# A dense projection stage with weight pieces made the moving operand, 512 columns at a time

## The chip, the cores and the metric

One NeuronCore of one Trainium2 chip runs the whole program. The metric is device time in microseconds of one execution, lower is better. Before the change the median of three runs is 1664.23 us (1663.21 to 1665.11).

## What is computed

One decoder layer over 256 tokens of width 2048, everything in float32:

```
h = x @ w_in                        # 2048 -> 9216: u, v, q, k, vb, gate_a, gate_b
v = LayerNorm(gelu(hv)); ya = (gelu(hu) * (tril(W_s) v + b_s)) @ w_out_a
ob = stick_breaking_attention(q, k, vb) @ w_out_b           # 8 heads of 128
x = LayerNorm(alpha*x + (sigmoid(ga)*ya + sigmoid(gb)*ob) @ w_o)
x = LayerNorm(alpha*x + top2_of_16_experts(x) + sigmoid(x @ w_g) * (p @ w_p))
```

The change touches the first four lines, called the dense part below. The router, the experts and the last norm keep their code.

## The kernel before

**Pieces.** Every dense weight is streamed from HBM once, in 2 MB tiles of 128 partitions by 4096 floats, through a pool of 12 such tiles that also holds activations (`B`, `load_one`, `prefetch`, lines 45 to 147). A load is issued on SP's queue as soon as a tile comes free (`done`). A tile is cut into eight pieces of 128x512. `split_next` (lines 235 to 252) turns each piece into two parts in the float32r format: ACT copies the piece into `hi` (L247), DVE subtracts to get `lo` (L248). Four piece buffers (`pc`) rotate, and `next_piece` keeps three pieces ahead of TensorE.

**Products.** A float32 product is made of three float32r products, hi*hi, hi*lo and lo*hi. A piece holds two 128-row chunks of 256 output columns, and costs 12 matmuls of 256 moving columns, in one of two forms. In `ws_piece` (L261) the 128x128 weight block is stationary and 256 tokens move, so the result comes out transposed (channels on partitions, tokens along the free dimension). In `xs_piece` (L275) a block of 128 tokens is stationary and 256 weight columns move, so the result has tokens on partitions. `block` runs eight pieces into one PSUM bank.

**Order.** vb (xs), then q and k alternating (ws), v (xs), u (ws), then eight rounds of gate_a, gate_b, w_out_a, w_out_b (all ws), then w_o (xs). After every second piece `pop_bg` issues one entry of a queue of small background jobs: attention steps `att1`, `att2`, `att3`, the norm of v, and `gate` (L413), which makes the causal product of one head, adds a bias that varies along the free dimension (`bsB`), multiplies by `uT`, and splits the result into `yax`. Each merge round ends with two DVE products, one POOL sum (L449) and an ACT/DVE split into `mixh`, `mixl`.

**Behind it.** After w_o come the norm, the router and the expert loop (L722, L748), which also streams 2 MB tiles.

Of the kernel before, what the change touches and what calls it, by code (L numbers as in the profile page):

```python
# [8 lines left out]
F32 = mybir.dt.float32  # L9
# [4 lines left out]
OP = mybir.AluOpType  # L14
# [18 lines left out]
def trunk(ctx, tc, I, out):  # L33
# [22 lines left out]
    def MM():  # L56
        return psum.tile([128, 512], F32, name="mm", tag="mm")
# [12 lines left out]
    def spec(key, parts):  # L70
        loads.append((key, parts))
# [3 lines left out]
    def spec_in(kind, i, base):  # L75
        spec((kind, i), [(slice(0, 4096), w_in[base + i].rearrange("p c f -> p (c f)"))])

    for i in range(4):
        spec_in("vb", i, 16)
    for i in range(4):  # L80
        spec_in("q", i, 8)
        spec_in("k", i, 12)
    for i in range(4):
        spec_in("v", i, 4)
    for i in range(4):
        spec_in("u", i, 0)
    for i in range(8):
        spec_in("ga", i, 20)
        spec_in("gb", i, 28)
        spec(("ab", i), [(slice(0, 2048), w_oa[i].rearrange("p c f -> p (c f)")),  # L90
                         (slice(2048, 4096), w_ob[i].rearrange("p c f -> p (c f)"))])
    for i in range(8):
        spec(("wo", i), [(slice(0, 4096), w_o[i].rearrange("p c f -> p (c f)"))])
# [73 lines left out]
    for a, b in ((0, 2), (2, 4), (4, 8), (8, 12), (12, 16)):  # L167
        s = slice(a * 256, b * 256)
        SP.dma_start(xr[:, s], I["xT"][:, a:b, :].rearrange("p c t -> p (c t)"))
        SP.dma_start(w0[:, s], w_in[16, :, a:b, :].rearrange("p c f -> p (c f)"))  # L170
    tiles["vb", 0] = w0
    w1 = B("w1")
    for i in range(4):
        SP.dma_start(w1[:, i * 1024:(i + 1) * 1024], w_in[17, :, 4 * i:4 * i + 4, :].rearrange("p c f -> p (c f)"))
    tiles["vb", 1] = w1
# [41 lines left out]

    vbv = B("vbv").rearrange("p (k a f) -> p k a f", k=2, a=2)
# [16 lines left out]
    def split_next():  # L235
        i = psplit["i"]
        if i >= len(psplit["list"]):
            return
        k, p = psplit["list"][i]
        psplit["i"] += 1  # L240
        if p == 0:
            cur[k] = take(k)
        if k == ("vb", 0):
            xsplit(2 * p)
        w = cur[k][:, p * 512:(p + 1) * 512]
        hi, lo = pc[:, 0, i % 4, :], pc[:, 1, i % 4, :]
        ACT.activation(hi, w, AF.Copy)  # L247
        DVE.tensor_sub(lo, w, hi.bitcast(F32))  # L248
        if p == 7:
            cur.pop(k)  # L250
            done()
        pieces.append((hi.rearrange("p (c f) -> p c f", c=2), lo.rearrange("p (c f) -> p c f", c=2)))
# [8 lines left out]
    def ws_piece(ps, p, rh, rl, first, last, c0):  # L261
        hi, lo = next_piece()
        n = 0
        for c in range(2):
            for j in range(2):
                js = slice(j * 128, (j + 1) * 128)
                o = ps[:, j * T:(j + 1) * T]
                for l, r in ((hi, rh), (hi, rl), (lo, rh)):
                    PE.matmul(o, l[:, c, js], r[:, c0 + c, :], start=(first and n == 0),  # L269
                              stop=(last and c == 1 and l is lo), skip_group_check=True)  # L270
                    n += 1
        if p % 2:
            pop_bg()

    def xs_piece(ps, p, sh, sl, first, last, c0):  # L275
        hi, lo = next_piece()
        n = 0
        for c in range(2):
            for a in range(2):
                as_ = slice(a * 128, (a + 1) * 128)  # L280
                o = ps[:, a * 256:(a + 1) * 256]
                for l, r in ((sh, hi), (sh, lo), (sl, hi)):
                    PE.matmul(o, l[:, c0 + c, as_], r[:, c, :], start=(first and n == 0),  # L283
                              stop=(last and c == 1 and l is sl), skip_group_check=True)
                    n += 1
        if p % 2:
            pop_bg()

    def block(f, ops_h, ops_l):
        ps = MM()  # L290
        for p in range(8):
            f(ps, p, ops_h, ops_l, p == 0, p == 7, 2 * p)
        return ps

    plan([("vb", i) for i in range(4)])
    for i in range(4):
        plan([("q", i), ("k", i)])
    plan([("v", i) for i in range(4)])
    plan([("u", i) for i in range(4)])
    for i in range(8):  # L300
        plan([("ga", i), ("gb", i), ("ab", i)])
    plan([("wo", i) for i in range(8)])
# [45 lines left out]
    for i in range(4):  # L348
        ps = block(xs_piece, xh, xl)
        DVE.tensor_copy(vbv[:, 0, :, i * 256:(i + 1) * 256], ps.rearrange("p (a f) -> p a f", a=2))  # L350
    for i in range(4):
        ps = block(ws_piece, xh, xl)
        ACT.activation(qk[:, 0, 2 * i:2 * i + 2, :].rearrange("p h t -> p (h t)"), ps, AF.Copy, scale=SCALE)
        ps = block(ws_piece, xh, xl)
        DVE.tensor_copy(qk[:, 1, 2 * i:2 * i + 2, :].rearrange("p h t -> p (h t)"), ps)
        att_bg(2 * i)
    state["reserve"] = 1
    for i in range(4):
        ps = block(xs_piece, xh, xl)
        DVE.tensor_copy(vbv[:, 1, :, i * 256:(i + 1) * 256], ps.rearrange("p (a f) -> p a f", a=2))  # L360
# [5 lines left out]
    uT = ug[:, 0:2048].rearrange("p (h t) -> p h t", h=NH)  # L366
# [5 lines left out]
    bsB = vbv[:, 0, 1, :].rearrange("p (h t) -> p h t", h=NH)  # L372
    SP.dma_start(wsT, I["gmlp_ws"])
    SP.dma_start(bsB.rearrange("p h t -> p (h t)"), I["gmlp_bs"].to_broadcast([128, 1024]))
# [34 lines left out]
    for i in range(4):  # L409
        ps = block(ws_piece, xh, xl)  # L410
        ACT.activation(uT[:, 2 * i:2 * i + 2, :].rearrange("p h t -> p (h t)"), ps, AF.Gelu_apprx_tanh)

    def gate(h):  # L413
        f = AUX()
        for a in range(2):
            PE.matmul(f[:, a * 128:(a + 1) * 128], v[:, a, h * 128:(h + 1) * 128], wsT[:, h, :],
                      start=True, stop=True)
        y = S("y")
        DVE.tensor_tensor(y[:, 0:256].rearrange("p (a t) -> p a t", a=2),
                          f[:, 0:256].rearrange("p (a t) -> p a t", a=2),  # L420
                          bsB[:, h:h + 1, :].to_broadcast([128, 2, 128]), op=OP.add)
        DVE.tensor_mul(y[:, 0:256], y[:, 0:256], uT[:, h, :])
        ACT.activation(yax[:, 0, h, :], y[:, 0:256], AF.Copy)
        DVE.tensor_sub(yax[:, 1, h, :], y[:, 0:256], yax[:, 0, h, :].bitcast(F32))

    drain()
    for h in range(NH):
        bg.append(lambda h=h: gate(h))
# [3 lines left out]
    for i in range(8):  # L432
        sg = []
        for k in range(2):
            ps = block(ws_piece, xh, xl)
            t = S("sg")
            ACT.activation(t, ps, AF.Sigmoid)
            sg.append(t)
        if i == 0:
            drain()  # L440
            free(2)
            mixh = B("mixh", F32R).rearrange("p (c t) -> p c t", c=DC)
            mixl = B("mixl", F32R).rearrange("p (c t) -> p c t", c=DC)
        for k, src in ((0, yax), (1, obx)):
            ps = MM()
            for p in range(4):
                ws_piece(ps, p, src[:, 0], src[:, 1], p == 0, p == 3, 2 * p)
            DVE.tensor_mul(sg[k], sg[k], ps)
        POOL.tensor_add(sg[0], sg[0], sg[1])  # L449
        mh = mixh[:, 2 * i:2 * i + 2, :].rearrange("p c t -> p (c t)")  # L450
        ml = mixl[:, 2 * i:2 * i + 2, :].rearrange("p c t -> p (c t)")
        ACT.activation(mh, sg[0], AF.Copy)
        DVE.tensor_sub(ml, sg[0], mh.bitcast(F32))
# [16 lines left out]
    lst = C("lst", [128, 2, 8, 6])  # L470
# [4 lines left out]
    for i in range(8):  # L475
        ps = block(xs_piece, mixh, mixl)
        xb = x1[:, :, i * 256:(i + 1) * 256]
        DVE.scalar_tensor_tensor(xb, xb, ALPHA, ps.rearrange("p (a f) -> p a f", a=2), op0=OP.mult, op1=OP.add)
        for a in range(2):
            DVE.bn_stats(lst[:, a, i, :], x1[:, a, i * 256:(i + 1) * 256])  # L480
        if i == 4:
            DVE.tensor_tensor(rwg, rw, gc[:, 0, :, None].to_broadcast([128, DC, 32]), op=OP.mult)
# [544 lines left out]
def _lay(inputs):  # L1027
    import numpy as np
    a = {k: np.asarray(v) for k, v in inputs.items()}

    def cols(w, c, n):
        return w.reshape(c, 128, n, 256).transpose(2, 1, 0, 3)
# [11 lines left out]
        "w_in": cols(a["w_in"][0], DC, 36),  # L1044
        "w_out_a": cols(a["w_out_a"][0], 8, 8),
        "w_out_b": cols(a["w_out_b"][0], 8, 8),
        "w_o": cols(a["w_o"][0], DC, 8),
# [3 lines left out]
        "gmlp_bs": a["gmlp_bs"].reshape(1, 1024),  # L1051
# [30 lines left out]
```

## Time and profile before

| | |
|---|---|
| median of three runs | 1664.23 us |
| profiled execution | 1663.73 us |
| its span, first to last instruction | 1661.70 us |
| dense part on TensorE | 5.35 to 629.3 us |
| router | 629.3 to 647 us |
| experts, last norm, output | 647 to 1661.7 us |

The span is what the trace covers; some 2 us lie around it. TensorE's matmuls overlap in the trace: one of 256 columns is shown with 0.28 us although the next starts 0.12 us later. The pace is therefore read from start to start, not from the duration. A float32 matmul is recorded as two instructions, a float32r one as one.

### The profile page before, as it was taken

To read this page: it belongs to the slowest core of one execution; us is meant where nothing else is said; L and a number is where in the kernel's file an instruction comes from. 1 tells how busy PE (TensorE), PEld (TensorE's weight loads), DVE (VectorE), ACT (ScalarE), POOL (GpSimd) and SP (SyncE) were. 2 spreads that over 40 slices of the span, in tenths; PEclk is the share of its full clock that TensorE was granted. 3 is DMA by queue.
4 is the path that set the end of the run, shared out by engine and by line. 5 is a ranking of instruction groups with operands and counts; after the bars stand their busy time and mean duration, and the time that the engine had idled before them with its cause. 6 is when DMAs were issued, how large, how long until landed. Compare 5 with 4: busy or idle time off the path is not lost. (4 is left out here: it accounts for less than half of the span.)

```text
span 1661.7 us, 23179 instructions
## 1 busy us (share of the span) xinstructions
PE 1616.9 (97%) x9974; PEld 1064.9 (64%) x9974; DVE 558.1 (34%) x1016; ACT 391.7 (24%) x696; POOL 38.6 (2%) x41
## 2 busy tenths in 40 slices
PE   8999999999999999999999999999999999999994
PEld 8999999999999995433333333553535535455323
DVE  5555576555555663120212131012010120101126
ACT  5455455444444441100001100000000000000001
POOL 0000000000000000000000000000000000000012
PEclk9999999999999999999999999999999999999997
DMA  9724553445546856999999999999998998998994
GB/s 387 322 102 153 207 199 129 176 165 190 192 164 254 316 195 263 394 412 414 428 427 428 427 428 427 427 426 424 387 429 374 381 427 375 428 382 373 429 387 173
DMA packets 44191, 540.94 MB, mean 326 GB/s; under 512 B 7090, under 2 KB 7090, under 8 KB 10546
## 3 DMA queue, kind: packets, MB, share of 16 engines
q1 hardware_dynamic: 44084, 539.42, 79.0%
q8 instruction: 79, 1.29, 0.3%
q14 instruction: 28, 0.23, 0.0%
HBM read 537.31 MB, written 2.10 MB: 325 GB/s over the span
## 5 line engine op out<-in xcount | busy, mean ns | idle before, releaser
L722 PE MATMUL mm<-w,xg 128*64 128x512 f32 x2048 | 460.9, 598 | 3.8 <-PEq L892 2.6
L248 DVE TENSOR_TENSOR pc<-w,pc 128x512 fp32r<-128x512 f32 x416 | 282.3, 691 | 211.0 <-ACT pc L247 206.8
L269 PE MATMUL mm<-xh,pc 128*128 128x256 f32 x1792 | 330.0, 284 | 0.0
L722 PEld LDWEIGHTS mm<-w,xg 128*64 128x64 f32 x2048 | 140.0, 137 | 264.4 <-issue 249.9
L247 ACT ACTIVATE pc<-w 128x512 fp32r<-128x512 f32 x416 | 256.1, 627 | 226.1 <-PE mm L269 129.4
L269 PEld LDWEIGHTS mm<-xh,pc 128*128 128x128 f32 x1792 | 281.7, 192 | 0.0
L269 PE MATMUL mm<-xl,pc 128*128 128x256 f32 x896 | 253.5, 283 | 0.0
L748 PE MATMUL mm<-w,hT 128*64 128x512 f32 x960 | 211.3, 595 | 0.0
L269 PEld LDWEIGHTS mm<-xl,pc 128*128 128x128 f32 x896 | 171.9, 192 | 0.0
L748 PEld LDWEIGHTS mm<-w,hT 128*64 128x64 f32 x960 | 66.8, 137 | 127.2 <-issue 126.4
L677 DVE TENSOR_SCALAR xg<-aux,gc 128x128 f32<-128x128 f32 x64 | 26.2, 409 | 318.2 <-ACT xg L676 318.2
L707 PE MATMUL mm<-w,x1T 128*128 128x256 f32 x512 | 111.8, 379 | 0.0
L707 PEld LDWEIGHTS mm<-w,x1T 128*128 128x128 f32 x512 | 97.3, 190 | 13.2
L283 PE MATMUL mm<-pc,xh 128*128 128x256 f32 x512 | 95.6, 288 | 6.0 <-ACT pc L247 5.3
L676 ACT ACTIVATE xg<-aux,gc 128x128 f32<-128x128 f32 x64 | 29.3, 457 | 287.1 <-PE aux L673 287.1
L673 PEld LDWEIGHTS aux<-P,x 128*128 128x128 f32 x512 | 61.9, 191 | 51.0 <-issue 50.3
L283 PE MATMUL mm<-pc,mixh 128*128 128x256 f32 x512 | 92.5, 283 | 0.3 <-DVE pc L248 0.3
L283 PEld LDWEIGHTS mm<-pc,xh 128*128 128x128 f32 x512 | 81.1, 194 | 7.0 <-ACT pc L247 5.6
L713 DVE TENSOR_TENSOR s<-s,aux 128x512 f32<-128x512 f32 x8 | 5.5, 688 | 238.5 <-ACT s L712 238.5
L283 PEld LDWEIGHTS mm<-pc,mixh 128*128 128x128 f32 x512 | 79.9, 192 | 0.5 <-DVE pc L248 0.5
L766 PE MATMUL aux<-misc 64*128 64x512 f32 x240 | 73.4, 629 | 2.6 <-DVE acc L775 2.5
L673 PE MATMUL aux<-P,x 128*128 128x128 f32 x512 | 73.8, 288 | 0.6 <-DVE P L639 0.6
(192 smaller groups left out, 1061.5 us busy)
## 6 DMA issues: line engine op xcount, KB each, us to landing
w<-in_exp_w_dram SPq DMA_DIRECT2D x188, 2048.0 KB, 14.2
w<-in_w_in_dram SPq DMA_DIRECT2D x34, 2048.0 KB, 8.7
w<-in_w_o_dram SPq DMA_DIRECT2D x8, 2048.0 KB, 7.7
w<-in_ple_w_gate_dram SPq DMA_DIRECT2D x8, 2048.0 KB, 14.1
w<-in_w_out_a_dram SPq DMA_DIRECT2D x8, 1024.0 KB, 4.9
w<-in_w_out_b_dram SPq DMA_DIRECT2D x8, 1024.0 KB, 7.4
w<-in_exp_d_last_dram SPq DMA_DIRECT2D x4, 2048.0 KB, 30.4
w<-in_w_in_dram SPq DMA_DIRECT2D x7, 512.0 KB, 10.2
```

The source lines that it names most:

```text
L247: ACT.activation(hi, w, AF.Copy)
L248: DVE.tensor_sub(lo, w, hi.bitcast(F32))
L269: PE.matmul(o, l[:, c, js], r[:, c0 + c, :], start=(first and n == 0), stop=(last and c == 1 and l is lo), skip_group_check=True)
L283: PE.matmul(o, l[:, c0 + c, as_], r[:, c, :], start=(first and n == 0), stop=(last and c == 1 and l is sl), skip_group_check=True)
L673: PE.matmul(ps[:, j * 128:(j + 1) * 128], x1[:, a, c * 128:(c + 1) * 128], P[:, a, :], start=(a == 0), stop=(a == 1))
L676: ACT.activation(xg[:, c, :], ps[:, 0:128], AF.Identity, scale=gc[:, 0, c:c + 1], bias=gc[:, 1, c:c + 1])
L677: DVE.tensor_scalar(xg[:, c + 1, :], ps[:, 128:256], gc[:, 0, c + 1:c + 2], gc[:, 1, c + 1:c + 2], op0=OP.mult, op1=OP.add)
L707: PE.matmul(ps[:, a * 256:(a + 1) * 256], x1T[:, c, a * 128:(a + 1) * 128], w[:, c, :], start=(c == 0 and a == 0), stop=(c == DC - 1), ski ...
L713: DVE.tensor_mul(s, s, pw)
L722: PE.matmul(ps[64 * hf:64 * hf + 64, :], x, w[:, hf * 512:(hf + 1) * 512], start=(c == 0), stop=(c == DC - 1), skip_group_check=True, tile ...
L748: PE.matmul(py[b][64 * hf:64 * hf + 64, :], hT[:, fc % 4, fc // 4, :], w[:, hf * 1024 + b * 512:hf * 1024 + b * 512 + 512], start=(fc == 0 ...
L766: PE.matmul(ps, PT[64 * hf:64 * hf + 64, a * 128:(a + 1) * 128], y[b][64 * hf:64 * hf + 64, :], start=True, stop=True, tile_position=(64 * ...
```

## The change

All dense products take the form with tokens stationary and 512 weight columns moving. Weight tiles are laid out on the host as 512-column blocks in two halves of eight chunks, so that a piece is now one 128-row chunk of 512 columns. A block fills two PSUM banks, one for each half of the tokens. Results that are needed transposed (q, k, the gated y, the merged rows) are turned by TensorE transposes, four to a PSUM bank, issued as background jobs. The gate makes two heads at a time, with the bias as a per-partition scalar.

```diff
-    def ws_piece(ps, p, rh, rl, first, last, c0):
-        ...
-    def xs_piece(ps, p, sh, sl, first, last, c0):
-        ...
+    def mm_piece(ps, p, sh, sl, first, last, c):
         hi, lo = next_piece()
+        for a in range(2):
+            as_ = slice(a * 128, (a + 1) * 128)
+            for n, (l, r) in enumerate(((sh, hi), (sh, lo), (sl, hi))):
+                PE.matmul(ps[a], l[:, c, as_], r, start=(first and n == 0), stop=(last and n == 2))
         if p % 2:
             pop_bg()
+    def block(sh, sl, n=DC):
+        ps = [MM(), MM()]
+        for c in range(n):
+            mm_piece(ps, c, sh, sl, c == 0, c == n - 1, c)
+        return ps
+    def turn2(src):
+        ps = AUX()
+        for j in range(2):
             for a in range(2):
+                PE.transpose(ps[:, j * T + a * 128:j * T + (a + 1) * 128], src(a, j), ident)
         return ps
...
+    for i in range(2):                                    # q and k
+        for k in range(2):
+            ps = block(xh, xl)
+            ACT.activation(vbv[:, 1, 0, k * 512:(k + 1) * 512], ps[0], AF.Copy)
+            DVE.tensor_copy(vbv[:, 1, 1, k * 512:(k + 1) * 512], ps[1])
+            bg.extend([lambda k=k, i=i, m=m: turn_qk(k, i, m) for m in range(2)])
+        att_bg(4 * i)
+        att_bg(4 * i + 2)
...
     def gate(h):
         f = AUX()
+        y = ys[h] = S("y")
+        for j in range(2):
+            for a in range(2):
+                PE.matmul(f[:, j * T + a * 128:j * T + (a + 1) * 128], wsT[:, h + j, :],
+                          v[:, a, (h + j) * 128:(h + j + 1) * 128], start=True, stop=True)
+        for j in range(2):
+            js = slice(j * T, (j + 1) * T)
+            DVE.scalar_tensor_tensor(..., bsT[:, h + j:h + j + 1],
+                                     u[:, :, (h + j) * 128:(h + j + 1) * 128], op0=OP.add, op1=OP.mult)
+    def split_turned(ps, h, l):
+        ACT.activation(h, ps, AF.Copy)
+        DVE.tensor_sub(l, ps, h.bitcast(F32))
+    for h in range(0, NH, 2):
+        bg.extend([lambda h=h: gate(h), lambda h=h: gate_turn(h)])
...
+    for i in range(4):                                    # merge rounds, were 8
...
+        for a in range(2):
+            POOL.tensor_add(sg[a], sg[a], sg[2 + a])
+        bg.extend([None] + [lambda sg=sg, i=i, m=m: mix_turn(sg, i, m) for m in range(2)])
...
+    for i in range(4):                                    # w_o, was 8
+        ps = block(mixh, mixl)
         for a in range(2):
+            xb = x1[:, a, i * 512:(i + 1) * 512]
+            DVE.scalar_tensor_tensor(xb, xb, ALPHA, ps[a], op0=OP.mult, op1=OP.add)
+            DVE.bn_stats(lst[:, a, i, :], xb)
...
-        if k == ("vb", 0):
-            xsplit(2 * p)
+        if k[:2] == ("vb", 0) and p % 2 == 0:
+            xsplit(8 * k[2] + p)
```

`turn_qk`, `gate_turn` and `mix_turn` each call `turn2` once and evacuate its bank with ACT and DVE. The first loads are reordered so that the first block's pieces (256 KB each) arrive with two chunks of x for every two pieces; before it was two chunks of x for each piece.

## Rows read from the trace of the kernel before

**Rows 1.** The page: its head, TensorE in part 1, two lines of part 2.
```profile
span 1661.7 us, 23179 instructions
PE 1616.9 (97%) x9974; PEld 1064.9 (64%) x9974; DVE 558.1 (34%) x1016; ACT 391.7 (24%) x696; POOL 38.6 (2%) x41
...
PEclk9999999999999999999999999999999999999997
DMA  9724553445546856999999999999998998998994
```
**Rows 2.** Windows by stage: busy us (instructions) of each engine, granted clock, DMA share, GB/s.
```profile
5.35:629.30 623.95, 622.94 (x5136) 620.38 (x5136) 355.50 (x566) 299.99 (x508) 12.81 (x10) 1.00 0.55 210
629.30:647.00 17.70, 16.49 (x146) 9.84 (x145) 11.27 (x39) 5.02 (x9) 0.70 (x1) 1.00 0.73 297
647.00:1661.70 1014.70, 977.42 (x4697) 434.67 (x4695) 189.34 (x402) 84.18 (x177) 24.14 (x16) 0.99 0.95 398
...
640.00:650.00 10.00, 9.23 (x54) 4.74 (x54) 6.34 (x33) 1.14 (x3) 0.00 (x0) 1.00 0.23 95
```
**Rows 3.** Waits of TensorE from 0 to 650 us: total, times, longest.
```profile
PE mm L283 <- ACT pc L247: 5.3, 1, 5.3
PE mm L283 <- DVE pc L248: 0.7, 2, 0.3
```
**Rows 4.** Waits of SP's queue over the span, the longest in total.
```profile
SPq L129 <- DVE pc L248: 530.3, 45, 27.4
```
**Rows 5.** Groups by line: the splits of the 416 pieces.
```profile
L248 DVE TENSOR_TENSOR pc<-w,pc 128x512 fp32r<-128x512 f32 x416 | 282.3, 691 | 211.0 <-ACT pc L247 206.8
...
L247 ACT ACTIVATE pc<-w 128x512 fp32r<-128x512 f32 x416 | 256.1, 627 | 226.1 <-PE mm L269 129.4
```
**Rows 6.** Timeline of TensorE at the dense part's end (start, us, count).
```profile
621.75 0.40 PE L283 MATMUL mm<-pc,mixh 128*128 128x256 f32 x2
621.99 0.28 PE L283 MATMUL mm<-pc,mixl 128*128 128x256 f32 x1
...
629.19 0.28 PE L283 MATMUL mm<-pc,mixl 128*128 128x256 f32 x1
...
630.50 2.33 PE L495 MATMUL aux<-ones_b 128*128 128x512 bf16 x10
```
**Rows 7.** Timeline of TensorE in the router and expert part: plain float32 products.
```profile
645.47 2.02 PE L673 MATMUL aux<-P,x 128*128 128x128 f32 x16 [0.65 <-DVE P L639]
...
1037.78 9.44 PE L707 MATMUL mm<-w,x1T 128*128 128x256 f32 x43
```
**Rows 8.** Timeline of TensorE, its first matmuls.
```profile
5.35 1.31 PE L283 MATMUL mm<-pc,xh 128*128 128x256 f32 x2 [5.35 <-ACT pc L247]
6.46 0.41 PE L283 MATMUL mm<-pc,xl 128*128 128x256 f32 x1
...
7.74 0.41 PE L283 MATMUL mm<-pc,xl 128*128 128x256 f32 x1
...
8.59 1.15 PE L283 MATMUL mm<-pc,xh 128*128 128x256 f32 x2
...
11.74 0.39 PE L283 MATMUL mm<-pc,xh 128*128 128x256 f32 x1 [0.34 <-DVE pc L248]
```
**Rows 9.** Timeline of TensorE where small groups stand between others.
```profile
259.33 0.28 PE L269 MATMUL mm<-xh,pc 128*128 128x256 f32 x1
259.45 0.61 PE L416 MATMUL aux<-vbv 128*128 128x128 f32 x4
...
260.01 0.28 PE L269 MATMUL mm<-xl,pc 128*128 128x256 f32 x1
...
888.81 0.66 PE L502 MATMUL aux<-ident,x 128*128 128x128 f32 x4
889.39 3.65 PE L722 MATMUL mm<-w,xg 128*64 128x512 f32 x16
```
**Rows 10.** Timeline of POOL: the last merge round's sum.
```profile
537.60 1.29 POOL L449 TENSOR_TENSOR sg<-sg 128x512 f32<-128x512 f32 x1 [33.27 <-DVE sg L448]
```

More of the change, by code (lines that the diff above doesn't have):

```diff
@@ L73, in trunk, with spec_in, spec_half, both @@
     w_in, w_oa, w_ob, w_o = I["w_in"], I["w_out_a"], I["w_out_b"], I["w_o"]
-    def spec_in(kind, i, base):
-        spec((kind, i), [(slice(0, 4096), w_in[base + i].rearrange("p c f -> p (c f)"))])
-    for i in range(4):
-        spec_in("vb", i, 16)
-    for i in range(4):
[L81 to L93, printed above, removed]
+    def spec_in(kind, base, n):
+        for i in range(n):
+            for kh in range(2):
+                spec((kind, i, kh), [(slice(0, 4096), w_in[base + i, kh].rearrange("p c f -> p (c f)"))])
+    def spec_half(kind, i, w):
+        spec((kind, i), [(slice(0, 4096), w[i, 0].rearrange("p c f -> p (c f)"))])
+    def both(kind, i):
+        return [(kind, i, kh) for kh in range(2)]
+    spec_in("vb", 8, 2)
+    for i in range(2):
+        for kind, base in (("q", 4), ("k", 6)):
+            for kh in range(2):
+                spec((kind, i, kh), [(slice(0, 4096), w_in[base + i, kh].rearrange("p c f -> p (c f)"))])
+    spec_in("v", 2, 2)
+    spec_in("u", 0, 2)
+    for i in range(4):
+        for kind, base in (("ga", 10), ("gb", 14)):
+            for kh in range(2):
+                spec((kind, i, kh), [(slice(0, 4096), w_in[base + i, kh].rearrange("p c f -> p (c f)"))])
+        spec_half("oa", i, w_oa)
+        spec_half("ob", i, w_ob)
+    for i in range(4):
+        for kh in range(2):
+            spec(("wo", i, kh), [(slice(0, 4096), w_o[i, kh].rearrange("p c f -> p (c f)"))])
     xw, xd = I["exp_w"], I["exp_d_last"]
@@ L166, in trunk, with head @@
     w0 = B("w0")
[L167 to L171, printed above, removed]
-    w1 = B("w1")
-    for i in range(4):
-        SP.dma_start(w1[:, i * 1024:(i + 1) * 1024], w_in[17, :, 4 * i:4 * i + 4, :].rearrange("p c f -> p (c f)"))
-    tiles["vb", 1] = w1
+    w1 = B("w1")
+    def head(t, lo, hi, src):
+        n = 256 if t is xr else 512
+        SP.dma_start(t[:, lo * n:hi * n], src[:, lo:hi, :].rearrange("p c f -> p (c f)"))
+    for a, b in ((0, 2), (2, 4), (4, 8)):
+        head(xr, a, b, I["xT"])
+        if a == 0:
+            head(w0, 0, 1, w_in[8, 0])
+            head(w0, 1, 2, w_in[8, 0])
+        else:
+            head(w0, a, b, w_in[8, 0])
+    for a, b in ((0, 4), (4, 8)):
+        head(xr, 8 + a, 8 + b, I["xT"])
+        head(w1, a, b, w_in[8, 1])
+    tiles["vb", 0, 0], tiles["vb", 0, 1] = w0, w1
     state["next"] = state["out"] = 2
@@ L251, in split_next @@
             done()
-        pieces.append((hi.rearrange("p (c f) -> p c f", c=2), lo.rearrange("p (c f) -> p c f", c=2)))
+        pieces.append((hi, lo))
     LA = 3
@@ L259, in next_piece @@
         return pieces.popleft()
-    def ws_piece(ps, p, rh, rl, first, last, c0):
+    def mm_piece(ps, p, sh, sl, first, last, c):
         hi, lo = next_piece()
[L263 to L271, printed above, removed]
+        for a in range(2):
+            as_ = slice(a * 128, (a + 1) * 128)
+            for n, (l, r) in enumerate(((sh, hi), (sh, lo), (sl, hi))):
+                PE.matmul(ps[a], l[:, c, as_], r, start=(first and n == 0), stop=(last and n == 2))
@@ L272, in ws_piece @@
         if p % 2:
             pop_bg()
-    def xs_piece(ps, p, sh, sl, first, last, c0):
-        hi, lo = next_piece()
-        n = 0
-        for c in range(2):
-            for a in range(2):
[L280 to L292, printed above, removed]
-        return ps
[L295 to L302, printed above, removed]
+    def block(sh, sl, n=DC):
[3 more added lines that the diff above has]
+        return ps
@@ L305, in trunk @@
+    for kind in ("vb0", "vb1", "q0", "k0", "q1", "k1", "v0", "v1", "u0", "u1"):
+        plan(both(kind[:-1], int(kind[-1])))
+    for i in range(4):
+        plan(both("ga", i) + both("gb", i) + [("oa", i), ("ob", i)])
+    for i in range(4):
+        plan(both("wo", i))
+    def turn2(src):
+        ps = AUX()
+        for j in range(2):
+            for a in range(2):
+                PE.transpose(ps[:, j * T + a * 128:j * T + (a + 1) * 128], src(a, j), ident)
+        return ps
     hs = {}
@@ L346, in att_bg, with turn_qk @@
                    lambda: att3(h0), lambda: att3(h1)])
[L348 to L356, printed above, removed]
-    state["reserve"] = 1
-    for i in range(4):
-        ps = block(xs_piece, xh, xl)
-        DVE.tensor_copy(vbv[:, 1, :, i * 256:(i + 1) * 256], ps.rearrange("p (a f) -> p a f", a=2))
+    def turn_qk(k, i, m):
+        ps = turn2(lambda a, j: vbv[:, 1, a, k * 512 + (2 * m + j) * 128:k * 512 + (2 * m + j + 1) * 128])
+        o = qk[:, k, 4 * i + 2 * m:4 * i + 2 * m + 2, :].rearrange("p h t -> p (h t)")
+        if k:
+            DVE.tensor_copy(o, ps)
+        else:
+            ACT.activation(o, ps, AF.Copy, scale=SCALE)
+    for i in range(2):
+        ps = block(xh, xl)
+        ACT.activation(vbv[:, 0, 0, i * 512:(i + 1) * 512], ps[0], AF.Copy)
+        DVE.tensor_copy(vbv[:, 0, 1, i * 512:(i + 1) * 512], ps[1])
+    for i in range(2):
+        for k in range(2):
+            ps = block(xh, xl)
+            ACT.activation(vbv[:, 1, 0, k * 512:(k + 1) * 512], ps[0], AF.Copy)
[3 more added lines that the diff above has]
+        att_bg(4 * i + 2)
+    state["reserve"] = 1
+    for i in range(2):
+        ps = block(xh, xl)
+        if i == 0:
+            while len(bg) > 8:
+                pop_bg()
+        ACT.activation(vbv[:, 1, 0, i * 512:(i + 1) * 512], ps[0], AF.Copy)
+        DVE.tensor_copy(vbv[:, 1, 1, i * 512:(i + 1) * 512], ps[1])
     drain()
@@ L365, in trunk @@
     ug = B("ug")
-    uT = ug[:, 0:2048].rearrange("p (h t) -> p h t", h=NH)
+    u = ug[:, 0:2048].rearrange("p (a f) -> p a f", a=2)
     lng = ug[:, 2048:3072]
@@ L371, in trunk @@
     wsT = vbv[:, 0, 0, :].rearrange("p (h t) -> p h t", h=NH)
-    bsB = vbv[:, 0, 1, :].rearrange("p (h t) -> p h t", h=NH)
     SP.dma_start(wsT, I["gmlp_ws"])
-    SP.dma_start(bsB.rearrange("p h t -> p (h t)"), I["gmlp_bs"].to_broadcast([128, 1024]))
+    bsT = C("bsT", [128, NH])
+    SP.dma_start(bsT, I["gmlp_bs"])
     POOL.affine_select(wsT, wsT, pattern=[[0, NH], [1, 128]], compare_op=OP.is_ge, fill=0.0, base=0,
@@ L407, in trunk @@
     bg.extend([lambda a=a, k=k: v_norm(a, k) for a, k in two])
-    for i in range(4):
-        ps = block(ws_piece, xh, xl)
-        ACT.activation(uT[:, 2 * i:2 * i + 2, :].rearrange("p h t -> p (h t)"), ps, AF.Gelu_apprx_tanh)
+    for i in range(2):
+        ps = block(xh, xl)
+        for a in range(2):
+            ACT.activation(u[:, a, i * 512:(i + 1) * 512], ps[a], AF.Gelu_apprx_tanh)
+    ys = {}
     def gate(h):
         f = AUX()
[L415 to L424, printed above, removed]
+        y = ys[h] = S("y")
[5 more added lines that the diff above has]
+            js = slice(j * T, (j + 1) * T)
+            DVE.scalar_tensor_tensor(y[:, js].rearrange("p (a f) -> p a f", a=2),
+                                     f[:, js].rearrange("p (a f) -> p a f", a=2), bsT[:, h + j:h + j + 1],
+                                     u[:, :, (h + j) * 128:(h + j + 1) * 128], op0=OP.add, op1=OP.mult)
@@ L426, in trunk, with gate_turn @@
+    def split_turned(ps, h, l):
+        ACT.activation(h, ps, AF.Copy)
+        DVE.tensor_sub(l, ps, h.bitcast(F32))
+    def gate_turn(h):
+        y = ys.pop(h)
+        ps = turn2(lambda a, j: y[:, j * T + a * 128:j * T + (a + 1) * 128])
+        split_turned(ps, *(yax[:, k, h:h + 2, :].rearrange("p h t -> p (h t)") for k in range(2)))
     drain()
-    for h in range(NH):
-        bg.append(lambda h=h: gate(h))
+    for h in range(0, NH, 2):
+        bg.extend([lambda h=h: gate(h), lambda h=h: gate_turn(h)])
@@ L431, in trunk, with mix_turn @@
     mixh = mixl = None
-    for i in range(8):
+    def mix_turn(sg, i, m):
+        ps = turn2(lambda a, j: sg[a][:, (2 * m + j) * 128:(2 * m + j + 1) * 128])
+        c = 4 * i + 2 * m
+        split_turned(ps, *(t[:, c:c + 2, :].rearrange("p c t -> p (c t)") for t in (mixh, mixl)))
+    for i in range(4):
         sg = []
         for k in range(2):
[L435 to L438, printed above, removed]
+            ps = block(xh, xl)
+            for a in range(2):
+                t = S("sg")
+                ACT.activation(t, ps[a], AF.Sigmoid)
+                sg.append(t)
@@ L444, in trunk @@
         for k, src in ((0, yax), (1, obx)):
[L445 to L453, printed above, removed]
+            ps = block(src[:, 0], src[:, 1], 8)
+            for a in range(2):
+                DVE.tensor_mul(sg[2 * k + a], sg[2 * k + a], ps[a])
+        for a in range(2):
+            POOL.tensor_add(sg[a], sg[a], sg[2 + a])
+        bg.extend([None] + [lambda sg=sg, i=i, m=m: mix_turn(sg, i, m) for m in range(2)])
     free(4)
@@ L469, in trunk @@
     DVE.memset(rbias, 0.0)
-    lst = C("lst", [128, 2, 8, 6])
+    lst = C("lst", [128, 2, 4, 6])
     lmv = C("lmv", [128, 2, 2])
@@ L473, in trunk @@
     lnm = C("lnm", [128, 2])
[L475 to L478, printed above, removed]
+    for i in range(4):
+        ps = block(mixh, mixl)
         for a in range(2):
-            DVE.bn_stats(lst[:, a, i, :], x1[:, a, i * 256:(i + 1) * 256])
-        if i == 4:
+            xb = x1[:, a, i * 512:(i + 1) * 512]
+            DVE.scalar_tensor_tensor(xb, xb, ALPHA, ps[a], op0=OP.mult, op1=OP.add)
+            DVE.bn_stats(lst[:, a, i, :], xb)
+        if i == 2:
             DVE.tensor_tensor(rwg, rw, gc[:, 0, :, None].to_broadcast([128, DC, 32]), op=OP.mult)
@@ L1029, in _lay, with halves @@
     a = {k: np.asarray(v) for k, v in inputs.items()}
+    def halves(w, n):
+        return w.reshape(-1, 8, 128, n, 512).transpose(3, 0, 2, 1, 4)
     def cols(w, c, n):
@@ L1043, in _lay @@
         "pT": a["p"][0, 0].reshape(T, 2, 128).transpose(2, 1, 0),
[L1044 to L1047, printed above, removed]
+        "w_in": halves(a["w_in"][0], 18),
+        "w_out_a": halves(a["w_out_a"][0], 4),
+        "w_out_b": halves(a["w_out_b"][0], 4),
+        "w_o": halves(a["w_o"][0], 4),
         "ple_w_gate": cols(a["ple_w_gate"][0], DC, 8),
@@ L1050, in _lay @@
         "gmlp_ws": a["gmlp_ws"][0].transpose(2, 0, 1),
-        "gmlp_bs": a["gmlp_bs"].reshape(1, 1024),
+        "gmlp_bs": a["gmlp_bs"][0].T,
         "gmlp_ln_g": a["gmlp_ln_g"],
```

## The prediction

> **What bounds the kernel now.** I read the page first. TensorE is busy 97% of the span and its clock stands at full speed in nearly every slice, while DMA is at 0.9 and more only from the sixteenth slice on [rows 1]. So there are two stages with different limits. The windows by stage put the border at 629.3 us: before it DMA is at 0.55 and DVE works 355.5 of 623.95 us, behind it DMA is at 0.95 for 1014.7 us [rows 2]. The waits tell that the dense part is TensorE's: it waits 5.3 us for its first piece and later 0.7 us in all [rows 3]. SP's queue, on the other hand, waits 530.3 us for splits to give tiles back [rows 4], so the loads are ahead and held up by full buffers. What is taken out of TensorE's stream here is taken out of the time, if the expert part starts in the same state.
>
> The stream itself is 416 pieces [rows 5] of 12 matmuls, 4992 in all. From 621.75 to 629.19 us there are 62 starts (two, one, two, one and so on, to the last), so 7.44 / 62 = 0.120 us from start to start [rows 6]. 4992 x 0.120 = 599.0 us of the 623.95.
>
> **The pace at 512 columns: the term that decides.** The change makes 6 matmuls of 512 columns out of 12 of 256; the columns streamed stay the same. So it gains only what a matmul costs beyond its columns. At the upper of the clock's two levels, 2.4 GHz, 256 columns are 0.1067 us, so 0.0133 us of the 0.120 is something else. No row has float32r matmuls of another length, so the new pace is bounded by what this excess may be.
>
> - It belongs to each matmul: 0.2133 + 0.0133 = 0.2267 us. 2496 x 0.2267 = 565.8 us, 33.2 less.
> - It vanishes behind the longer stream. The nearest matmuls with 512 steps and a new stationary block each are the float32 ones at L707, (9.44 - 0.38) / 42 = 0.2157 us [rows 7], and the bfloat16 ones at L495, (2.33 - 0.38) / 9 = 0.217 us [rows 6]. 2496 x 0.2157 = 538.4 us, 60.6 less.
> - It belongs to each column, as when four bytes a step cannot be fed at full rate: 0.240 us, 599.0 us, nothing gained.
>
> Two rows speak to this. In the first microseconds six matmuls start between 6.46 and 7.74 us, 0.213 us each [rows 8], which is 256 columns at 1.2 GHz with no excess at all; I go by this pace for the lower clock level, an inference. So the excess is not a number of array cycles but something beside the array that only a fast array meets. All three readings allow that. Then the plain float32 products: with 256 steps (128x128 at L673) they take (2.02 - 0.29) / 15 = 0.115 us, 0.009 over the pure steps, and with 512 steps 0.2157, 0.002 over [rows 7]. There the excess does not grow with the length. It speaks against the third reading, though these forms need a new float only every second step. I take the first: -33.2 us. It is in the middle of the bounds, and it needs no assumption that something hides.
>
> TensorE's page of the Trainium skill (TensorE: Matmul & The Clock Gate, Back-to-back issue gap) gives N/2.4 + 2.5 ns for a matmul of N columns. That would be 109 ns at 256, where the rows above show 120, and 216 ns at 512, the second reading; the measured 120 says the rule misses something in this form. The page SBUF — State Buffer (A bandwidth-pool intuition that's wrong) speaks against the change: it gives the moving operand a port of two bytes a lane at 2.4 GHz. Taken as it stands, 256 four-byte columns would need 0.213 us, which 0.120 contradicts; but a port that limits by bytes is the third reading.
>
> **The turns: added.** 20 groups of four transposes (8 for q and k, 4 for y, 8 for the merged rows). Transposes between float32r matmuls don't occur before. The nearest row is a group of four 128x128 float32 products in the same stream: from the matmul before it to the second one behind it are 260.01 - 259.33 = 0.68 us [rows 9], 0.24 of which are two matmuls of 0.120, so 0.44 us. Four transposes among expert products take 889.39 - 888.81 = 0.58 us [rows 9]. Lower end 0.43, the pure steps; they cannot cost less, since TensorE has no idle time to put them in. I take 0.44, the same neighbours: 20 x 0.44 = +8.8 us, up to 11.6.
>
> **The gate by pairs: moved.** 16 products in four groups of eight where there were eight of four: the same float32 work on TensorE, 0. Two DVE operations a head become one, and the bias is no longer a 128x256 operand; DVE has 43% idle time to hide either.
>
> **Evacuations and waits.** A block's result is now two banks, emptied by ACT and DVE side by side in the 0.63 and 0.69 us of such an operation [rows 5]; that work and the turned banks' sit behind TensorE, which has three split pieces in hand, 3 x 6 x 0.227 = 4.1 us. A turn waits for its source. q and k: emptied about 1 us after the block, turned two pieces (2.7 us) later. y: two DVE operations, then two pieces later. Merged rows: two DVE products and two POOL sums of 1.29 us [rows 10] in a row, 0.2 + 0.7 + 2.6 = 3.5 us; the empty slot puts the turn four pieces behind, 5.4 us. Without that slot the turn would come at 2.7 us, and TensorE with everything behind it would wait 0.8 us in each of four rounds. The last turns must be split before w_o reads chunks 12 to 15, piece 12 of 16; they are issued after pieces 3 and 5. Cost 0; at worst 1 us a round, 4 us. Splits per piece stay at 0.69 us of DVE against 1.36 us of TensorE.
>
> **SP's queue and the loads.** Tiles are of the same size and number in the dense part, in the same order of use; w_out_a and w_out_b become one load a tile instead of two halves. Fewer queue entries, nothing later. 109 MB in 26 us less lifts the share from 0.55 to about 0.57.
>
> **The start.** Before, each piece needed 256 KB of weight and 256 KB of x. The 26th matmul starts at 11.74 us (18 lines, of which the first, the last and three between stand in [rows 8]), where 5.35 + 25 x 0.12 would be 8.35, so 3.4 us are lost to waits and the slow clock. Now a piece needs half the x. The slow clock stays, some of the waits between 8.59 and 11.74 should go: I take -1.1 us, a third of the loss, 0 to -2.
>
> **Sum.** -33.2 + 8.8 - 1.1 = -25.5 us on TensorE's stream, the dense part ending near 603.8 us. The expert part shifts with it: from 640 to 650 us DMA is at 0.23 [rows 2], so the tiles were full before experts began, with some 8 us of idle DMA to spare, and the 14 us of transfers that the lost time held (25.5 x 0.55) spread over a stage whose DMA is 45% idle. The profiled execution is 1663.73 us (span 1661.7 and 2.0 around it), 0.5 below the median. 1663.7 - 25.5 = 1638.2.
>
> **Rivals.**
> - The excess hides entirely: -60.6 + 8.8 - 1.1 = -52.9, 1611 us. For it: both 512-step rows. Against: neither feeds four bytes a step.
> - The stream is fed by columns: +8.8 - 1.1 = +7.7, 1671 us, up to 1674 with turns of 0.58. Its place is every matmul of the dense part; it decides from a pace of 0.237 up, where 599.0 - 2496 x 0.237 = 7.5 us no longer pays for the turns less the start. For it: four bytes a step is the only thing that sets this form apart from the float32 one with the same steps and the same weight load. Against: the excess of the other forms does not grow with length.
> - The stream gets faster and the gain is lost behind it: the expert part, at 0.95 of DMA, starts with emptier buffers, or turns make TensorE wait for DVE. Between 1645 and 1664 us. For it: DMA is the next limit. Against: the idle DMA at 640 us, and DVE at 57%.
>
> **How the numbers follow.** Forecast 0.52, hidden excess 0.21, fed by columns 0.17, lost behind 0.10. 0.2% (3.3 us) is about what a measurement of this kernel can tell from no change. Faster: the first two and half of the last, 0.78. Within 0.2%: 0.06, from the last and from paces near 0.237. Slower: 0.16. The forecast's own range is 1630 to 1646. The range from 1608 to 1660 takes in the hidden excess and most of the last, and leaves out the case fed by columns.
>
> **What would show it.** The start-to-start time of the new line's matmuls: 0.227 right, 0.216 or 0.240 a rival. A group of turns: 0.44 us between its neighbours. The last dense matmul near 604 us and the first expert product about 18 us behind it. TensorE's waits in the dense part still under 2 us behind the first. DMA in the last 10 us ahead of the experts still well under full. If the expert part takes more than 1017 us, the state was not handed over.

## The result, and the profile after

The changed kernel takes 1643.72 us (median of four runs, 1642.69 to 1644.23); the kernel before took 1664.67 us beside it. The ratio is 0.9875, with a 95% interval of 0.9857 to 0.9892, so the change saves some 21 us. The forecast was 1638, 25.5 us less. The profiled execution took 1642.69 us, 21.0 us under that of before. In it line 283 is the one line of all dense matmuls, L264 and L265 are the splits, L306 is the turn's transpose, L757 the experts' gate and up product.

The page of the changed kernel, the lines that answer to [rows 1]:

```profile
span 1641.0 us, 18130 instructions
PE 1595.6 (97%) x7558; PEld 941.1 (57%) x7558; DVE 559.9 (34%) x996; ACT 400.0 (24%) x700; POOL 40.0 (2%) x41
...
PEclk9999999999999999999999999999999999999997
DMA  9743544255557767999999999999998999999994
```

Windows by stage, columns as in [rows 2]: the dense part, the router, the experts with what follows, and ten microseconds ahead of and into the experts.

```profile
5.37:606.99 601.62, 601.04 (x2720) 496.87 (x2720) 356.61 (x547) 308.21 (x512) 14.17 (x10) 1.00 0.57 216
606.99:625.71 18.72, 17.16 (x148) 10.14 (x146) 12.33 (x41) 5.12 (x9) 0.71 (x1) 1.00 0.69 295
625.71:1640.96 1015.25, 977.44 (x4693) 434.08 (x4692) 189.10 (x402) 84.17 (x176) 24.19 (x16) 0.99 0.95 398
...
618.00:628.00 10.00, 9.22 (x56) 4.73 (x54) 6.06 (x32) 1.15 (x3) 0.00 (x0) 1.00 0.19 78
```

The gain lies in the first stage alone. From the first dense matmul's start to the last one's it was 623.84 us and is 601.62. The two stages behind it are a little longer: 18.24 to 18.72 and 1014.3 to 1015.25 us. DMA ahead of the experts is at 0.19, as idle as before, so they begin with full buffers.

TensorE at the end of the dense part, beside [rows 6]:

```profile
603.13 0.61 PE L283 MATMUL mm<-pc,mixh 128*128 128x512 f32 x2
603.58 0.39 PE L283 MATMUL mm<-pc,mixl 128*128 128x512 f32 x1
...
606.98 0.39 PE L283 MATMUL mm<-pc,mixl 128*128 128x512 f32 x1
...
611.51 2.19 PE L578 MATMUL mm<-ident,x 128*128 128x128 f32 x16 [0.77 <-DVE x L557]
```

17 starts in 3.85 us: 0.2265 us each, where the first reading had 0.2267. The last line shows the router's first transposes waiting 0.77 us for DVE, whose chain behind the last block has grown: two sums and two statistics over 512 columns follow each other.

In the first microseconds the pace is another one:

```profile
6.69 0.63 PE L283 MATMUL mm<-pc,xl 128*128 128x512 f32 x1
...
9.25 0.55 PE L283 MATMUL mm<-pc,xl 128*128 128x512 f32 x1
```

Six starts in 2.56 us are 0.4267 us each, 512 columns at 1.2 GHz and nothing beside them, as the prediction read it at 256 columns. The level is inferred from this pace: the column of the granted clock reads 1.00 there as well.

TensorE around a group of turns (the gate's y), beside the group of four in [rows 9]:

```profile
275.93 0.39 PE L283 MATMUL mm<-pc,xl 128*128 128x512 f32 x1
276.16 0.60 PE L306 MATMUL aux<-ident,y 128*128 128x128 f32 x4
276.51 0.70 PE L283 MATMUL mm<-pc,xh 128*128 128x512 f32 x2
277.06 0.40 PE L283 MATMUL mm<-pc,xl 128*128 128x512 f32 x1
```

From 275.93 to 277.06 us there are three dense matmuls and the group: 1.13 - 3 x 0.227 = 0.45 us for four transposes. A transpose is recorded as one instruction; the float32 products of [rows 9] are two instructions each, so the group of four there is two products.

All start times of the dense part's matmuls, sorted into terms, close the account (us):

```
                                   before    after   difference
dense matmuls at 0.120 / 0.2267    598.92   565.53    -33.39
turns, 20 groups                     -        8.94     +8.94
gate, attention groups              21.08    21.23     +0.15
waits and slow clock at the start    3.50     3.11     -0.39
later waits for split pieces         0.59     1.32     +0.73
other departures from the pace      -0.25     1.49     +1.74
first to last dense matmul         623.84   601.62    -22.22
router                              18.24    18.72     +0.48
experts to the end                1014.30  1015.25     +0.95
```

### The profile page after: what moved, and what is told of

Its sections match the earlier page's. It is cut to its first block, busy times and chain, and to the rows that moved or that the text cites. A ratio compares the mean times of both kernels' runs of the same rounds, so it can differ in the third digit from the quotient of the medians.

```text
span 1641.0 us, 18130 instructions
## 1 busy us (share of the span) xinstructions
PE 1595.6 (97%) x7558; PEld 941.1 (57%) x7558; DVE 559.9 (34%) x996; ACT 400.0 (24%) x700; POOL 40.0 (2%) x41
## 5 line engine op out<-in xcount | busy, mean ns | idle before, releaser
L757 PE MATMUL mm<-w,xg 128*64 128x512 f32 x2048 | 461.3, 598 | 4.4 <-PEq L927 2.6
L283 PE MATMUL mm<-pc,xh 128*128 128x512 f32 x1152 | 362.8, 395 | 6.0 <-ACT pc L264 5.4
L265 DVE TENSOR_TENSOR pc<-w,pc 128x512 fp32r<-128x512 f32 x416 | 290.9, 710 | 198.9 <-ACT pc L264 196.3
L264 ACT ACTIVATE pc<-w 128x512 fp32r<-128x512 f32 x416 | 259.7, 630 | 233.4 <-DVE pc L265 179.8
L757 PEld LDWEIGHTS mm<-w,xg 128*64 128x64 f32 x2048 | 139.7, 137 | 265.8 <-issue 249.7
L283 PEld LDWEIGHTS mm<-pc,xh 128*128 128x128 f32 x1152 | 213.8, 189 | 51.2 <-ACT pc L264 5.9
L283 PE MATMUL mm<-pc,xl 128*128 128x512 f32 x576 | 225.4, 391 | 0.0
L283 PEld LDWEIGHTS mm<-pc,xl 128*128 128x128 f32 x576 | 108.5, 188 | 22.9
L283 PE MATMUL mm<-pc,mixh 128*128 128x512 f32 x256 | 79.0, 390 | 0.0
L810 DVE TENSOR_TENSOR acc<-acc,aux 128x512 f32<-128x512 f32 x112 | 68.4, 680 | 14.8 <-PE aux L801 14.8
L767 DVE TENSOR_TENSOR s<-s,mm 128x256 f32<-128x256 f32 x32 | 13.4, 418 | 160.3 <-ACT s L766 160.3
L794 ACT ACTIVATE misc<-mm 128x512 f32<-128x512 f32 x30 | 17.7, 597 | 182.4 <-PE mm L783 182.4
```

Of the source, the lines that this page charges most:

```text
L283: PE.matmul(ps[a], l[:, c, as_], r, start=(first and n == 0), stop=(last and n == 2))
L757: PE.matmul(ps[64 * hf:64 * hf + 64, :], x, w[:, hf * 512:(hf + 1) * 512], start=(c == 0), stop=(c == DC - 1), skip_group_check=True, tile ...
L794: ACT.activation(y[-1], p, AF.Copy)
L810: DVE.tensor_add(xb, xb, pss[hf])
```

## The experiments

The main question was what the 0.0133 us that a matmul takes beyond its columns belongs to, since the forecast chose among three readings. The others test the waits that were costed at nothing.

**Rows of matmuls of other sizes.**

```diff
+    def probe(m, n, rows=128, plain=False):
+        ps = AUX()
+        for c in range(24):
+            l, r = mixh[0:rows, c % DC, 0:m], mv[0:rows, c % 7 * 512:c % 7 * 512 + n]
+            if plain:
+                l, r = l.bitcast(F32), r.bitcast(F32)
+            PE.matmul(ps[0:m, 0:n], l, r, start=True, stop=True)
+    probe(128, 512); probe(128, 384); probe(128, 256); probe(128, 128)
+    probe(64, 256); probe(32, 256); probe(128, 256, rows=64)
+    probe(128, 256, plain=True); probe(128, 128, plain=True)
```

> Ten rows of 24 matmuls each are put between w_o and the router, into PSUM banks that nobody reads; the rest is the changed kernel. Theory A (each float32r matmul costs its columns at 2.4 GHz plus 13.3 ns, whatever its length): start to start 0.2267 us at 512 columns, 0.173 at 384, 0.120 at 256, 0.067 at 128 unless the weight load sets a floor near 0.11 there; the same 0.120 at 256 columns with 64 or 32 stationary columns. Rival B (the excess is the reading of the next stationary block, which shrinks with that block): 0.113 with 64 stationary columns and 0.110 with 32. Rival C (the excess is a share of the columns, and the 0.227 seen at 512 has another cause): 0.18 at 384. Plain float32 at 256 columns 0.216, at 128 columns 0.109 to 0.112; bfloat16 at 256 columns 0.109 if the excess is float32r's own.

Windows of TensorE in this kernel, from the first start of one row of 24 to the first start of the next (the count in brackets takes in what is still in flight at the edges): 512, 384, 256 and 128 columns, then 256 columns with 64 stationary columns, 23 starts with 32, 22 starts with 64 rows, and plain float32 at 128 columns, which is 48 instructions:

```profile
607.41:612.85 5.44, 5.44 (x26) 1.00 0.98 410
612.85:617.03 4.18, 4.18 (x25) 1.00 0.60 251
617.03:619.90 2.87, 2.87 (x26) 1.00 0.00 0
619.90:622.53 2.63, 2.63 (x27) 1.00 0.00 0
622.53:625.27 2.74, 2.74 (x27) 1.00 0.00 0
625.27:627.88 2.61, 2.61 (x26) 1.00 0.00 0
628.30:630.94 2.64, 2.64 (x24) 1.00 0.00 0
...
641.61:646.97 5.36, 5.36 (x50) 1.00 0.00 0
```

And the bfloat16 row of the timeline:

```profile
646.96 2.78 PE L539 MATMUL aux<-ones_b 128*128 128x256 bf16 x24
```

Divided: 0.2267 at 512 columns, 0.174 at 384, 0.120 at 256 and 0.110 at 128. From 256 to 512 that is 0.107 us for 256 columns, the pure column time, and 0.013 at either length. Theory A holds from 256 up; at 128 a floor of 0.110 takes over, near the 0.112 of plain float32 there. Rival C (0.18 at 384) is out: the 0.174 is a mean over a row whose first eight steps are uneven (0.171 to 0.185 us), and the last fifteen are 0.173 each. Rival B holds in half: with 64 stationary columns 0.114, but with 32 still 0.1135, so half of the excess goes when the block is halved and no more after that. With 64 rows instead of 128 it is 0.120, unchanged. bfloat16 takes (2.78 - 0.27) / 23 = 0.109. So some 0.0025 us stands in bfloat16 too, as in plain float32 of 256 columns (0.2157 us, [rows 7]); the rest is float32r's, and somewhat more than half of that rest, 0.0065 of 0.011 us, hangs on a stationary block of more than 64 columns. Why is left open. So is whether the excess belongs to the matmul or to the load of its block: each of the dense part's matmuls has a load of its own (2720 and 2720 instructions in the windows above), and no run reuses a loaded block.

**The change with matmuls of 256 columns.**

```diff
-                PE.matmul(ps[a], l[:, c, as_], r, ...)
+                for f in range(2):
+                    fs = slice(f * 256, (f + 1) * 256)
+                    PE.matmul(ps[a][:, fs], l[:, c, as_], r[:, fs], ...)
```

> The changed kernel with every 512-column product issued as two of 256 columns, the stationary block loaded for each; all else of the change stays. Theory A: 4992 matmuls of 0.120 instead of 2496 of 0.2267, +33 us on the changed kernel, about 1677 us, so slower than before the change by the turns (some 9 to 12 us). Rival (part of the gain comes from the layout, the start or the evacuations, not from the matmuls' length): clearly under 1670 us.

Measured: 1672.92 us, ratio to the kernel before 1.0056 (1.0039 to 1.0072). All the change without its length is slower by 9 us. TensorE at its end:

```profile
631.07 0.64 PE L285 MATMUL mm<-pc,mixh 128*128 128x256 f32 x4
631.55 0.40 PE L285 MATMUL mm<-pc,mixl 128*128 128x256 f32 x2
...
637.31 0.40 PE L285 MATMUL mm<-pc,mixl 128*128 128x256 f32 x2
```

52 starts in 6.24 us, 0.120. The dense part is 632.2 us, 8.4 over that of before, against 8.8 of turns in its trace. It is 30.6 us over the changed kernel's, 33.4 of them the stream; of the 2.8 given back, the norm stalls (1.1) and the matmuls behind a group (2.0), both below, are the most, and the start, 0.6 us longer in this trace, goes the other way. The expected 1677 was 4 us too high, most of it for that reason. This run changes only the length of the matmuls, and with it the gain is gone.

**Without the empty entry ahead of the merged rows' turns.**

```diff
-        bg.extend([None] + [lambda sg=sg, i=i, m=m: mix_turn(sg, i, m) for m in range(2)])
+        bg.extend([lambda sg=sg, i=i, m=m: mix_turn(sg, i, m) for m in range(2)])
```

> The changed kernel without the empty entry ahead of the turns of the merged rows. The prediction's step says TensorE then waits 0.8 us for POOL's sums in each of four rounds, +3.2 us; by the changed kernel's trace, where the sums end 1.5 us ahead of the turn and the turn would come 2.7 us earlier, it is 1.2 us a round, +4.9 us. Rival: the other jobs give the slack and nothing changes, within 1 us.

Measured: 1648.25 us, 4.5 us over the changed kernel's median, ratio 0.9906 (0.989 to 0.9923). TensorE around the first turn of a round, and its waits in this kernel:

```profile
323.38 0.39 PE L283 MATMUL mm<-pc,xl 128*128 128x512 f32 x1
323.61 0.27 PE L306 MATMUL aux<-ident,sg 128*128 128x128 f32 x1
324.84 0.55 PE L306 MATMUL aux<-ident,sg 128*128 128x128 f32 x3 [0.96 <-POOL sg L487]
325.14 0.72 PE L283 MATMUL mm<-pc,xh 128*128 128x512 f32 x2
```
```profile
PE aux L306 <- POOL sg L487: 3.7, 4, 1.0
```

The group's first transpose reads the first sum, the second waits for the other one. The four rounds cost 4.56 us more on TensorE's starts, 1.14 each. The mechanism is as foreseen, the price was 0.8 a round because the sums were taken at 1.29 us each; two in a row stand in the changed kernel's trace with 3.0, the second of them with about 1.75:

```profile
520.07 3.00 POOL L487 TENSOR_TENSOR sg<-sg 128x512 f32<-128x512 f32 x2 [63.26 <-DVE sg L485]
```

**Room between the norm jobs of v.**

```diff
-    bg.extend([lambda a=a, k=k: v_norm(a, k) for a, k in two])
+    for a, k in two:
+        bg.extend([lambda a=a, k=k: v_norm(a, k), None])
```

> The changed kernel with an empty entry behind each of the four norm jobs of v. Theory (three DVE operations of a norm job and two splits do not fit into two pieces, so TensorE runs out of split pieces between 227 and 235 us, three stalls of 1.1 us in all): these stalls go, -1.1 us. Rival (the stalls come from ACT, which also has the two gelu evacuations of u there): they stay or move.

The stalls stand in the waits of the changed kernel between 226 and 236 us (on the weight-load side of TensorE), and DVE's timeline shows the cause: three operations of a norm job and then two splits in a row.

```profile
PEld mm L283 <- DVE pc L265: 1.5, 3, 0.5
```
```profile
225.56 0.54 DVE L420 TENSOR_SCALAR vbv<-vbv,vmv,vrs 128x512 f32<-128x512 f32 x1
...
226.13 0.69 DVE L421 TENSOR_TENSOR vbv<-vbv,ug 128x512 f32<-128x512 f32 x1
226.86 0.69 DVE L422 TENSOR_TENSOR vbv<-vbv,ug 128x512 f32<-128x512 f32 x1
...
227.47 1.29 DVE L265 TENSOR_TENSOR pc<-w,pc 128x512 fp32r<-128x512 f32 x2
```

A job and two splits are 0.54 + 0.69 + 0.69 + 1.29 = 3.2 us, and two pieces are 12 x 0.227 = 2.7 us. Measured: 1641.73 us, ratio 0.9867 (0.9851 to 0.9884). In its trace the six late starts between 227 and 235 us are gone, 1.07 us. Whether the time follows can't be told: the interval spans the changed kernel's ratio, and in the profiled execution the start lost as much more. The rival (ACT) is out for these stalls. One of 0.25 us at 281 us stays, and that one is ACT's: it loads a table there (1.28 us) and makes two sigmoids before it comes back to the splits. The other pairs of sigmoids, without a table load, leave no stall.

```profile
277.41 1.28 ACT L475 ACT_TABLE_LOAD   x1
278.71 1.09 ACT L475 ACTIVATE sg<-mm 128x512 f32<-128x512 f32 x2
```

**The changed kernel again, beside the next three.** No edit.

> The changed kernel again, as the partner of the three runs beside it. Every theory: 20 to 22 us under the kernel before, 2496 matmuls at 0.2267 us, 20 groups of turns at 0.45 us.

Measured: 1643.64 us, ratio 0.9877 (0.986 to 0.9893). In its profiled execution the start costs 3.5 us where the first one's cost 3.1. In all traces of kernels with this same start it is 3.1 to 4.3 us (3.8 in the run without the empty entry, 4.3 in the one with room between the norm jobs).

**The gate for one head at a time.**

```diff
-        for j in range(2):
-            for a in range(2):
-                PE.matmul(f[:, j * T + a * 128:...], wsT[:, h + j, :], v[:, a, (h + j) * 128:...], ...)
+        for a in range(2):
+            PE.matmul(f[:, a * 128:(a + 1) * 128], wsT[:, h, :], v[:, a, h * 128:(h + 1) * 128], ...)
...
-        bg.extend([lambda h=h: gate(h), lambda h=h: gate_turn(h)])
+        bg.extend([lambda h=h: gate(h), lambda h=h: gate(h + 1), lambda h=h: gate_turn(h)])
```

> The changed kernel with the gate's products issued for one head at a time (eight jobs of four products instead of four of eight), the turns of y by pairs as they are. Theory: TensorE's work is the same and DVE's is hidden, so nothing changes, within 1 us. Rival (each interruption of the stream has a price of its own): four interruptions more, under 0.1 us each as the four-turn group costs 0.447 us for 4 x 0.109 of steps; at most +0.4 us.

Measured: 1642.88 us (1642.31 to 1645.23), ratio 0.9876 (0.986 to 0.9893), the same as the control within 1 us. On TensorE eight groups of two products (four instructions) cost 0.450 us each, 3.60 in all, where four groups of four products cost 0.897, 3.59. The interruption has no price of its own that shows here. (The expectation counts instructions where it says products.)

**TensorE warm before the first piece.**

```diff
+    ps = AUX()
+    for _ in range(6):
+        PE.matmul(ps, ones_b, ones_b[:, None, :].to_broadcast([128, 4, 128]), start=True, stop=True)
```

> The changed kernel with six bfloat16 matmuls on constants before the first piece arrives, while TensorE waits for its loads. Theory (part of the start's 2.7 us of loss is the lower clock level, 0.427 us a matmul until about 9.5 us): the pace is 0.227 us earlier, up to -1.4 us (seven matmuls of 0.2 us). Rival (the loads set the start): the time moves into waits for pieces and less than 0.5 us is left.

Measured: 1644.04 us, ratio 0.988 (0.9864 to 0.9897): nothing, the rival is right. TensorE's first microseconds in this kernel:

```profile
2.80 2.74 PE L214 MATMUL aux<-ones_b 128*128 128x512 bf16 x6 [2.80 <-DVE half L225]
...
8.48 0.39 PE L286 MATMUL mm<-pc,xl 128*128 128x512 f32 x1
10.30 0.50 PE L286 MATMUL mm<-pc,xh 128*128 128x512 f32 x1 [1.42 <-ACT pc L267]
```

The pace is 0.23 us from 6.4 us on, where the changed kernel keeps 0.427 until 9.25 us, and what it gains turns into 1.8 us between two starts at 8.48. The next piece, the third, is part of a load of two chunks that has not landed; ACT waits for it and splits it only here:

```profile
9.61 1.15 ACT L267 ACTIVATE pc<-w 128x512 fp32r<-128x512 f32 x2 [0.95 <-DMA w<-in_w_in_dram]
```

The moment differs between executions: in the changed kernel's trace this split begins at 8.80 us, in that of the run with room between the norm jobs at 9.68. That trace, without the early matmuls and with as late a load, loses 4.3 us at the start, this one 4.2.

**The version that the runs point to.** The room between the norm jobs and the six early matmuls as above, and the load of the first tile's last four chunks, with that of x beside it, in two parts:

```diff
-    for a, b in ((0, 2), (2, 4), (4, 8)):
+    for a, b in ((0, 2), (2, 4), (4, 6), (6, 8)):
```

> The empty entries behind the norm jobs, the six early matmuls, and the first loads of four chunks cut into two of two. Theory: -1.3 us for the norm stalls, -0.5 to -1.4 us at the start, so 2 to 3 us under the changed kernel. Rival: the start is set by the loads as a whole and only the norm's 1.3 us is left.

Measured: 1640.75 us (1640.33 to 1642.25), ratio 0.9862 (0.9845 to 0.9878), 2.9 us under the control. In its trace the start costs 2.4 us, 1.1 less than the control's, and the norm stalls are gone. Its four times all lie under the control's four (1643.34 to 1643.8), though the intervals of the two ratios overlap. What the early matmuls and the cut load each gave is not separated: the third piece still comes late (0.5 us between starts at 9.13 us), while the wait for the load of four, 0.75 us between starts at 13.44 us in the run with the early matmuls alone, is gone.

## Why the prediction was right

- **What bounds the dense part.** Right. 22.2 us out of TensorE's stream became 21 us of time, and 30.6 us put back into it by the 256-column run became 29.2.
- **The pace at 512 columns.** Right to the nanosecond, 0.2267 us, and the two bounds, 0.2157 and 0.240, are out. The argument behind it was weaker than the outcome: the excess is float32r's own for the most part, so the plain float32 rows [rows 7] were no evidence on it, and the size of the stationary block has a share in it.
- **The turns.** The price was right, 8.94 us for 8.8, and partly by luck. The row it came from was read as four float32 products; it is two, of two instructions each. Four transposes cost as much because a transpose is one instruction: 0.447 us for a group, four times the 0.112 us of a plain float32 instruction at 128 columns in the probe.
- **The gate by pairs.** Right: 3.59 us after, 3.58 before, and 3.60 for single heads. Its 16 products are 32 instructions; the groups of eight and four are instructions.
- **Evacuations and waits.** Costed at 0, 4 us at worst. For what was named (q and k, y, the merged rows, the last turns) it holds: TensorE has no wait at any turn. It failed for what was not named. The norm jobs of v did not change, but they are issued every second piece, and two pieces went from 2.88 to 2.72 us, so that three DVE operations and two splits no longer fit: 1.07 us, with 0.25 for ACT's table load and sigmoids at 281 us; a wait of 0.59 us of before is gone. Behind the last block DVE's chain became longer and the router starts 0.48 us later. The cover was there on average (DVE at 59%) and missing in one place.
- **The start.** -1.1 foreseen, -0.39 measured. With the same code the start lost 3.1 to 4.3 us in the traces, depending on when the third piece's load lands, so one trace on each side can't decide this term, and that it lies in its bounds, 0 to -2, says little.
- **Not foreseen: matmuls behind a group.** Behind an attention, gate or turn group some matmuls start 0.229 to 0.236 us apart instead of 0.2267; before they started 0.116 to 0.118 apart instead of 0.120. With what is spread over the other matmuls that is +1.74 us, 1.4 of them in the first eight matmuls behind a group. In the 256-column run they are again the faster ones. The cause was not found.
- **The state handed over.** Right, and the rival of a gain lost behind the dense part is out: the first six experts begin at 0, 57.0, 110.2, 162.6, 215.7 and 274.7 us of the expert part in both traces. The 0.95 us come later, 0.5 of them in the seventh expert, where TensorE waits for loads, and the term differs from run to run (the control 1.4 us over the kernel before, the best version 0.7). In the control's trace the sixth expert takes 3.0 us longer: the granted clock stands at 0.50 there from 940 to 946 us, behind a wait of TensorE for DVE of 1.4 us, which the first trace has too without the drop.
- **The sum.** -33.2 + 8.8 - 1.1 = -25.5 against -33.39 + 8.94 + 0.15 - 0.39 + 0.73 + 1.74 + 0.48 + 0.95 = -20.8 of span, and 0.3 less around it. Every term that was worked out from a row came within 0.7 us of it; the missing 4.5 us are 0.7 of the start and, for the rest, small terms of one sign that were costed at nothing.

## What to carry to other kernels

When a matmul costs its columns and a fixed amount besides, read the fixed amount from the start-to-start time and the column rate, and fill the bank with columns; what the longer form costs in added transposes is read from a group of small products in the same stream, counted in recorded instructions (here a float32 product is two and a transpose one). When the stream gets faster by a few per cent, look through the background jobs that are spaced by pieces of it for one whose helper engine was nearly full: the average load of that engine hides it. An early warm clock is worth nothing where the next load has not landed.

## What the runs showed of the hardware

- A float32r matmul with a 128x128 stationary block starts 0.0133 us plus its columns at 2.4 GHz after the one before, measured at 256, 384 (0.0142 on the mean of 24) and 512 columns; at the slower pace of the first microseconds there is no such excess (0.213 us at 256 columns, 0.4267 at 512); at 128 columns it does not get under 0.110. With 64 or 32 stationary columns and 256 moving ones it is 0.1135 to 0.114, with half the rows 0.120, bfloat16 0.109.
- A transpose of 128x128 float32 is recorded as one instruction and a group of four adds 0.447 us to the stream; a product of that size is two instructions, and four products add 0.897 us.
- The expert part is paced by TensorE and only in a few places by its loads, although DMA is at 0.95 there: its first five experts begin at 0, 57.0, 110.2, 162.6 and 215.7 us of it in the trace of every kernel run here, with the dense part ahead of it ending between 605 and 637 us. In the changed kernel's trace TensorE waits 1.8 us for the experts' weights and 1.8 for the last ones, and SP's queue 406 us for one of TensorE's lines alone:

```profile
PE mm L757 <- DMA w<-in_exp_w_dram: 1.8, 3, 1.2
PE mm L866 <- DMA w<-in_exp_d_last_dram: 1.8, 3, 0.7
SPq L137 <- PE mm L757: 406.3, 108, 8.4
```

- POOL's sum of 512 columns took 1.29 us alone and 3.0 us for two in a row.
